# The input of chunks 1 to 3 of a hybrid decoder layer: turned by VectorE from strided loads, with the norm's factor applied at the projections' outputs

## The chip, the cores and the metric

One core of one Trainium2 chip. The metric is device time in microseconds (us); the time before is 1935.48 us, the median of 3 runs (1933.53 to 1936.48).

## The reference

One layer on 2048 rows of 1024 float32 numbers. The layer's lines that matter:

```
h  = rms_norm(x, g)                      # x * rsqrt(mean(x*x) + eps) * g
z  = h @ w_in                            # q 512 | k 128 | v 128 | b 512 | c 512 | xc 512
A  = window attention(rms_norm(q), rms_norm(k), v, sinks)   # blocks of 128, 8 heads, 2 kv heads
Cv = b * short_conv(c * xc, conv_w)      # 3 taps, per column
x  = x + concat(rms_norm(A), rms_norm(Cv)) @ w_out
x  = x + square(relu(rms_norm(x) @ w_up)) @ w_down
```

rms_norm multiplies each row by one number and each column by one number. A row's number can therefore be left out ahead of `h @ w_in` and be multiplied into the rows of the product instead.

## The kernel before

Every product of two float32 matrices runs as three matmuls on parts: a high part, rounded to TensorE's format, and a low part, the rest (`mm3`, L264 to L268: high x high, high x low, low x high). Making the parts is one cast on ScalarE and one subtraction on VectorE.

The rows are worked through in four chunks of 512 (`mixers`, called for c = 0 to 3), each of four blocks of 128 (b = 0 to 15). `h` is the chunk's normalised input, turned so that its 1024 columns lie on the partitions: two tiles (high and low) of 128 x 8 x 512 with a single buffer, so that the next chunk's h is written when the last convolution group of this chunk has read it. A chunk has these pieces:

- The convolution, `conv_pair` (L779), twice per chunk: groups of 24 matmuls of 128x512 for two column tiles each of c (`pc`), xc (`px`) and b (`pb`). The result of pc is copied out of its PSUM bank (L803 on ScalarE; in chunk 0, where the row factor is not yet in h, L805 on VectorE multiplies by the squared factor `rs0_row`).
- The output projection, `out_projection`: half 1 (the convolution's rows, `pout` with `yt`) and half 0 (the attention's, `pout` with `at`). Each result is multiplied by the norm factor of its rows (`rc` or `ra`) and added to x (L892).
- The next chunk's input, `prepare` (L364): four fetches of 128 whole rows (512 KB each) into the two buffers `xt`; `norm` (squares on ScalarE, rsqrt on GpSimd, the multiplication by row factor and gain row on VectorE, L282); then `transposed` (L288): for every 128 rows, two groups of four TensorE transposes into one PSUM bank (L294), a cast to the high part (L298) and a subtraction for the low part (L299).
- The projection to q, k and v, `project_qkv`: `pz` groups of the next chunk.
- The attention of each block: q and k norm, `qk_transpose` (transposes ptq and ptk, L638 and L640, and their parts, L643 to L648), `softmax` (scores psc, L665, copies and selects L673 and L676, exponentials L682, normalisation L690), `values` (transposes of the probabilities ptp, L701, their parts pp, L707 and L708, window masks on GpSimd, L714, then po, L753, and o, L761 on), `attn_rstd` (one matmul pa, L774).

What sets the order: `besides` yields one small step at a time of convolution, output projection, preparation and projection, and `fill(n)` runs n such steps between the pieces of attention; the numbers are in FILL. That is the program's order. Below it a list scheduler of the tile framework builds the order on each engine from its own estimates of when operands are there, and a piece may be moved forward or back by a number from PRIO (`ahead(i)`). The built order is fixed: each engine runs its instructions in that order and waits at each for what it needs. PSUM has 3 banks for projections ("mm"), 4 for attention ("at"), 1 for transposes ("tr"). All loads, and the stores of weight parts that later chunks use, are issued from SyncE's (SP's) queue in program order.

The MLP follows the mixers, from about 700 us on. Its own input is turned by `load_turned` (L312: four strided loads, 32 x 32 x 32 pieces of 128 bytes) and `turned` (L321: a VectorE transposition within blocks of 32x32, L323, then a multiplication by gain and row factor, L325). `gain_row` (L356) loads one gain for all partitions.

Of the kernel before, what the change touches and what calls it, by code (L numbers as in the profile page):

```python
# [7 lines left out]
F32 = mybir.dt.float32  # L8
# [3 lines left out]
AF = mybir.ActivationFunctionType  # L12
# [4 lines left out]
P = 128  # L17
D = 1024
# [51 lines left out]
CHP = CH + 32  # L70
STEPS = 3
TS = 32
REST = 7
LATER = 250

# [27 lines left out]
def hymba_layer(  # L103
# [23 lines left out]

    const = ctx.enter_context(tc.tile_pool(name="const", bufs=1))
    small = ctx.enter_context(tc.tile_pool(name="small", bufs=1))

    both_pool = ctx.enter_context(tc.tile_pool(name="both", bufs=1, reuse_waits="tile"))
    wop_ctx = ExitStack()
# [16 lines left out]
        for tb in range(NTB)  # L149
    ]  # L150
    rs_dram = [dram.tile([CH], F32, name=f"rs_dram{c}") for c in range(NCHUNK)]
    wds_dram = [[dram.tile([P, 2, BW], F32, name=f"wds{g}_{i}") for i in range(2)] for g in range(NCG // 2)]

    def bank(tag, name):
# [126 lines left out]
    def scaled(xt, rs, gb):  # L281
        nc.vector.scalar_tensor_tensor(xt, xt, rs, gb, op0=ALU.mult, op1=ALU.mult)  # L282

    def norm(xt, gb, name):

        scaled(xt, norm_stats(xt, name), gb)

    def transposed(xt, dst, t, name, tag="tr"):  # L288

        for kk in range(0, KD, 4):  # L290
            with ahead(9):
                pt = bank(tag, f"pt_{name}_{kk}")
                for j in range(4):
                    nc.tensor.transpose(pt[:, j * P : (j + 1) * P], xt[:, (kk + j) * P : (kk + j + 1) * P], ident)  # L294
                p3 = pt.rearrange("p (k t) -> p k t", k=4)
                dh = dst[0][:, kk : kk + 4, t * P : (t + 1) * P]
                dl = dst[1][:, kk : kk + 4, t * P : (t + 1) * P]
                nc.scalar.copy(dh, p3)  # L298
                nc.vector.tensor_tensor(dl, p3, dh.bitcast(F32), op=ALU.subtract)  # L299
            yield  # L300

    def raised(xt, dst, name, tag="tr"):

        for k in range(2):
# [59 lines left out]
    def prepare(src, r0, gb, dst, name):  # L364

        xs = []

        def fetch(t):
            xt = row("xt", f"xt_{name}_{t}", 2)
            nc.sync.dma_start(xt, src[r0 + t * P : r0 + (t + 1) * P, :])  # L370
            with ahead(8):
                norm(xt, gb, f"{name}_{t}")
                xs.append(xt)

        fetch(0)
        fetch(1)
        yield
        for t in range(NT):
            yield from transposed(xs[t], dst, t, f"{name}_{t}")
            if t + 2 < NT:  # L380
                fetch(t + 2)


    def flat(blk):
        return blk.rearrange("p k c -> p (k c)")
# [158 lines left out]
    with tc.tile_pool(name="mix_small", bufs=1) as mix_small, tc.tile_pool(name="mix", bufs=1) as mix:  # L544
# [10 lines left out]
        def project_qkv(c, h, z):  # L555
# [36 lines left out]
            w4 = [w.rearrange("p (k c) -> p k c", k=KD) for w in weights(None, c, "qkv2")]  # L592

            for pc, t in ((0, 0), (0, 1), (1, 0), (0, 2), (0, 3), (1, 1), (1, 2), (1, 3)):
                n = 256 if pc else AW
                ps = bank("mm", f"pz{c}_{pc}_{t}")[:, :n]
                hk = lambda s, k, t=t: h[s][:, k, t * P : (t + 1) * P]
                wk = (lambda s, k: w4[s][:, k, :]) if pc else (lambda s, k: both[k // (KD // 2)][s][:, k % (KD // 2), :])
                for k in range(KD):
                    mm3(ps, lambda s, k=k: hk(s, k), lambda s, k=k: wk(s, k), k == 0, k == KD - 1)  # L600
                    if (k % 2 or not pc) and k < KD - 1:
# [174 lines left out]
            nc.vector.tensor_copy(ms, pa[:, :1])  # L776
            rsqrt(dst, ms)

        def conv_pair(c, h, j, yt, ssc):  # L779

            nm = f"c{c}_{j}"

# [15 lines left out]
            for i in range(2):  # L798
                ps = bank("mm", f"pc_{nm}_{i}")
                yield from group(hl, ps, i)  # L800
                g = pool.tile([P, CHP], F32, tag="s2", name=f"u_{nm}_{i}", bufs=4)
                if c:
                    nc.scalar.copy(g[:, 2 : CH + 2], ps)  # L803
                else:
                    nc.vector.tensor_tensor(g[:, 2 : CH + 2], ps, rs0_row, op=ALU.mult)  # L805
                gc.append(g)
                yield
            hl = weights(cols256(wi, O_X + j * 256), c, f"wx{j}")
# [129 lines left out]
                    x_put(0, t, 2, b[1])  # L938
                yield

        def besides(c, before, h, yt, rc, x1, h_next, z_next):
# [11 lines left out]
            out = out_projection(c, 1, yt, rc, x1)  # L953
            if c + 1 < NCHUNK:
                h_next += parts(pool, "h", f"h{c + 1}")
                steps = prepare(xf, (c + 1) * CH, g_row[0], h_next, f"a{c + 1}")
            else:
                steps = prepare_mlp(gain_row(mlp_norm_g, "g_mlp"))
            for i, _ in enumerate(steps):
                yield  # L960
                for j in range(STEPS):
                    next(out, None)
                    yield
                    if (i, j) == PC:
# [5 lines left out]
                        ms = mix_small.tile([P, NT], F32, tag="msc", name=f"ms_c{c}", bufs=1)  # L970

                        with tc.high_priority(offset=SOON):
                            if c:
                                nc.vector.tensor_copy(ms, pc[:, :NT])
                                rsqrt(rc, ms)
                            else:
                                nc.vector.tensor_tensor(ms, pc[:, :NT], rs0_2, op=ALU.mult)
                                rsqrt(rc, ms)
                                nc.gpsimd.tensor_tensor(rc, rc, rs0, op=ALU.mult)
            yield from out  # L980
            if c + 1 < NCHUNK:
                yield from project_qkv(c + 1, h_next, z_next)
            else:
                begin_mlp()

        def mixers(c, before, h, z):


            last = c + 1 == NCHUNK
            n_fill = FILL[c]  # L990
            stage[0] = c
            at, yt, x1, h_next, z_next = [], [], [], [], []
            ra = small.tile([P, NT], F32, tag="ra", name=f"ra{c}", bufs=2)
            rc = small.tile([P, NT], F32, tag="rc", name=f"rc{c}", bufs=2)
            steps = besides(c, before, h, yt, rc, x1, h_next, z_next)
            left = out_projection(c, 0, at, ra, x1)

            spare = (NT - 1) * NCT if last else 0
# [43 lines left out]
                        attn_rstd(b, sqa, ra[:, NT - 1 : NT])  # L1042
                    yield

            return rest(), h_next, z_next

        z = []
        for _ in project_qkv(0, h, z):
# [40 lines left out]
        left = iter(())  # L1089
        for c in range(NCHUNK):  # L1090
            left, h, z = mixers(c, left, h, z)
        for _ in left:
            pass

# [479 lines left out]
```

## Time and profile before

| | |
|---|---|
| median of 3 runs | 1935.48 us (1933.53 to 1936.48) |
| the profiled execution | 1936.33 us; its span, first to last instruction, 1934.6 us; granted clock 0.999 |
| transposes of chunks 1 to 3 | 96 in 24 groups of four |
| bytes moved by DMA | 412 MB, mean 213 GB/s |

PE is TensorE, PEld its weight load, DVE is VectorE, ACT is ScalarE, POOL is GpSimd, SP is SyncE. A line of a group reads: source line, engine, operation, output <- inputs, shape, count | busy us, mean ns of one | idle us of the engine just before them and what ended it. In the timeline: start, duration (us), engine, line, operation. SPq is the part of SyncE that issues transfers. Times are from one profiled execution.

### The profile page before, as it was taken

The numbers are of one execution on the slowest core, as the hardware profiler recorded it, in microseconds if no ns is written. First come the engines' busy times: TensorE is split into PE (matmuls) and PEld (weight loads), VectorE is DVE, ScalarE is ACT, GpSimd is POOL, SyncE is SP. The second block draws the span as 40 slices with busy tenths as digits, with TensorE's granted clock in tenths as the row PEclk, the third lists the DMA queues.
The fourth block names the chain that finished last, engine by engine and source line by source line (L and its number), as shares of the span: only waits on it lengthen the run. The fifth ranks groups of instructions, "written<-read, shape, count | busy, mean of one in ns | idle before, by whom it ended". The sixth has DMA issues, their size and how long they took to land.

```text
span 1934.6 us, 24806 instructions
## 1 busy us (share of the span) xinstructions
PE 1916.7 (99%) x9025; PEld 1596.0 (82%) x9025; DVE 1206.7 (62%) x1872; ACT 837.7 (43%) x1593; POOL 273.3 (14%) x473
## 2 busy tenths in 40 slices
PE   9999999999999999999999999999999999999999
PEld 9888888888888788888877888888888888888887
DVE  4885667447556768899878766666534334448541
ACT  6563445345344437445465554554422333232220
POOL 1112203312221112222201111101000000100000
PEclk9999999999999999999999999999999999999999
DMA  9774855464474787877665544437964457776631
GB/s 324 274 261 150 288 223 188 169 255 155 163 276 170 241 299 277 250 216 249 227 222 191 180 162 143 164 123 295 376 218 151 143 163 229 262 229 219 211 135 55
DMA packets 240634, 412.25 MB, mean 213 GB/s; under 512 B 51704, under 2 KB 147968, under 8 KB 228736
## 3 DMA queue, kind: packets, MB, share of 16 engines
q1 hardware_dynamic: 211824, 335.15, 51.3%
q0 software_dynamic: 15424, 51.40, 6.8%
q10 hardware_dynamic: 13264, 24.13, 3.3%
q8 instruction: 71, 1.16, 0.2%
q14 instruction: 51, 0.42, 0.1%
HBM read 284.78 MB, written 125.83 MB: 212 GB/s over the span
## 4 chain that ended last, share of the span: by engine, by line
PE 84%; issue 5%; DVE 4%; DMA 4%; ACT 2%; POOL 1%; SPq 1%; ACTq 0%; POOLq 0%; DVEq 0%
PE d L1534 31%; PE u L1427 23%; PE pout L266 2%; PE pout L268 2%; PE pout L267 2%; PE pz L266 2%; PE pz L267 2%; PE pz L268 2%; PE pc_c L266 2%; PE px_c L266 2%; PE px_c L267 2%; PE px_c L268 2%; PE pc_c L268 2%; PE pc_c L267 2%; PE psc_b L665 1%
## 5 line engine op out<-in xcount | busy, mean ns | idle before, releaser
L1427 PE MATMUL u<-op_x,wop 128*128 128x512 f32 x2688 | 612.5, 390 | 3.0 <-DVE wop L417 1.3
L1534 PE MATMUL d<-op_w,op_f 128*128 128x512 f32 x2688 | 609.4, 389 | 0.0
L1427 PEld LDWEIGHTS u<-op_x,wop 128*128 128x128 f32 x2688 | 503.7, 188 | 111.4 <-DVE wop L417 4.0
L1534 PEld LDWEIGHTS d<-op_w,op_f 128*128 128x128 f32 x2688 | 504.7, 188 | 104.6
L398 DVE TENSOR_TENSOR op_f<-op_f 128x1024 fp32r<-128x1024 f32 x112 | 136.9, 1225 | 237.8 <-ACT op_f L397 237.4
L397 ACT CAST op_f<-op_f 128x1024 fp32r<-128x1024 f32 x112 | 118.0, 1054 | 355.9 <-DMA op_f<-fop 343.7
L416 ACT CAST wop<-wu 128x512 fp32r<-128x512 f32 x156 | 96.4, 621 | 92.0 <-PE u L1427 87.7
L417 DVE TENSOR_TENSOR wop<-wu,wop 128x512 fp32r<-128x512 f32 x156 | 111.7, 717 | 34.1 <-ACT wop L416 19.0
L1163 POOL DMA_DIRECT2D fop<-s x96 | 52.3, 545 | 433.3 <-DVE s L1166 426.4
L1169 DVE TENSOR_TENSOR u<-u,u 128x512 f32<-128x512 f32 x128 | 87.8, 686 | 18.8 <-PE u L1427 18.8
L398 DVE TENSOR_TENSOR op_w<-raw,op_w 128x1024 fp32r<-128x1024 f32 x56 | 68.4, 1222 | 25.4 <-ACT op_w L397 25.4
L397 ACT CAST op_w<-raw 128x1024 fp32r<-128x1024 f32 x56 | 58.9, 1053 | 42.3 <-PE d L1534 20.1
L1175 ACT ACTIVATE u<-u 128x512 f32<-128x512 f32 x64 | 40.6, 634 | 51.7 <-DVE u L1169 50.0
L682 ACT ACTIVATE sc_b<-sc_b,ngm_b 128x128 f32<-128x128 f32 x128 | 49.9, 392 | 26.5 <-DVE ngm_b L679 26.5
L714 POOL TENSOR_SCALAR_AFFINE_SELECT pp_b<-pp_b 128x512 fp32r<-128x512 f32 x60 | 41.1, 697 | 116.9 <-ACT pp_b L707 63.4
L1376 POOL DMA_DIRECT2D wds<-raw x16 | 8.6, 535 | 333.8 <-DVE raw L1374 333.8
L416 ACT CAST wop<-wu_s 128x512 fp32r<-128x512 f32 x64 | 39.5, 621 | 35.6 <-PE u L1427 27.4
L266 PE MATMUL pout<-w_wo,yt_c 128*128 128x512 f32 x128 | 52.4, 410 | 0.0
L268 PE MATMUL pout<-w_wo,yt_c 128*128 128x512 f32 x128 | 51.9, 406 | 0.0
L267 PE MATMUL pout<-w_wo,yt_c 128*128 128x512 f32 x128 | 51.2, 400 | 0.0
L266 PE MATMUL pout<-w_wo,at_b 128*128 128x512 f32 x128 | 50.2, 395 | 0.2 <-DVE x L892 0.2
L267 PE MATMUL pout<-w_wo,at_b 128*128 128x512 f32 x128 | 50.0, 391 | 0.3 <-DVE w_wo L249 0.3
(255 smaller groups left out, 3132.7 us busy)
## 6 DMA issues: line engine op xcount, KB each, us to landing
op_f<-fop SPq DMA_DIRECT2D x112, 512.0 KB, 4.5
raw<-in_w_down_dram SPq DMA_DIRECT2D x72, 512.0 KB, 4.4
wu<-in_w_up_dram SPq DMA_DIRECT2D x128, 256.0 KB, 3.8
w_wo<-wo SPq DMA_DIRECT2D x24, 1024.0 KB, 6.8
fop<-s POOLq DMA_DIRECT2D x96, 256.0 KB, 2.7
fop<-u ACTq DMA_DIRECT2D x64, 256.0 KB, 2.3
op_x<-xop SPq DMA_DIRECT2D x28, 512.0 KB, 6.5
w_q<-qkv SPq DMA_DIRECT2D x24, 512.0 KB, 6.0
```

The costliest lines, as they stand in the source:

```text
L266: nc.tensor.matmul(ps, st(0), mv(0), start=first, stop=False)
L267: nc.tensor.matmul(ps, st(0), mv(1), start=False, stop=False)
L268: nc.tensor.matmul(ps, st(1), mv(0), start=False, stop=last)
L397: nc.scalar.copy(op[:, 0], raw)
L398: nc.vector.tensor_tensor(op[:, 1], raw, op[:, 0].bitcast(F32), op=ALU.subtract)
L416: splits.append(nc.scalar.copy(hi, blk).ins)
L417: nc.vector.tensor_tensor(lo, blk, hi.bitcast(F32), op=ALU.subtract)
L682: nc.scalar.activation(sc[:, hd, :], sc[:, hd, :], AF.Exp, bias=ngm[:, hd : hd + 1], accum_out=den[:, hd : hd + 1])
L1163: eng.dma_start(fop_dram[tb][ORDER_DOWN.index(i)][n // 2][:, n % 2], b)
L1169: return nc.vector.tensor_tensor(dst, ps, b, op=ALU.add).ins
L1427: nc.tensor.matmul(pt, wops[i][:, a, k, :], xops[tb, p][k // 2][:, b, k % 2, :], start=p not in GOES_ON and k + j == 0, stop=k + j == NB + ...
L1534: nc.tensor.matmul(ps[tb][j], fs[tb][:, a, k, j * P : (j + 1) * P], w[:, b, k, :], start=first and p not in GOES_ON and k + n == 0, stop=l ...
```

## The change

For chunks 1 to 3, `norm` and `transposed` are gone. `load_turned` brings x itself in blocks (four jj, each two column tiles k), VectorE turns them, and the parts of h are made with the column's gain as a per-partition number, without the row factor. The squares of the rows are taken from whole rows, loaded into the same two `xt` buffers earlier, during the convolution (`stats`, one step at every 13th convolution step). The row factor `rs` is applied where the q, k, v products are copied out of PSUM, its square at pc's output (from a row of squared factors stored to memory and loaded for all partitions), and the convolution's norm factor `rc` takes both as chunk 0's did. pc's output is now multiplied on VectorE in every chunk. The k loop of `project_qkv` goes in the order 0, 4, 1, 5, ... The gain row of the attention norm is gone; its buffer holds the turned tile and the row of squared factors. `small_pad` is an unused tile.

```
-                nc.scalar.copy(dh, p3)
-                nc.vector.tensor_tensor(dl, p3, dh.bitcast(F32), op=ALU.subtract)
...
+    def turned_input(c, jj):
+
+        xt = row("xt", f"xt_a{c}_{jj}", 2)
+        load_turned(xt, xf, c * CH, jj)
+        return xt
+
+    def prepare(c, dst, gb, xts):
+
+        yield
+        for jj in range(NB):
+            for k in (jj, jj + NB):
+                xt = xts[jj][:, (k // NB) * BW : (k // NB + 1) * BW]
+                with ahead(9):
+                    dh, dl = (d[:, k] for d in dst)
+                    st = gb[:, k // NB]
+                    nc.vector.transpose(st, xt)
+                    nc.scalar.activation(dh, st, AF.Copy, scale=g_in[k])
+                    nc.vector.scalar_tensor_tensor(dl, st, g_in[k], dh.bitcast(F32), op0=ALU.mult, op1=ALU.subtract)
+                yield
+            if jj + 2 < NB:
+                xts.append(turned_input(c, jj + 2))
+
+    def stats(c, rs, xts):
+
+        rows = []
+
+        def fetch(t):
+            r = c * CH + t * P
+            rows.append(row("xt", f"xr_a{c}_{t}", 2))
+            nc.sync.dma_start(rows[t], xf[r : r + P, :])
+
+        def square(t):
+            ss = small.tile([P, 1], F32, tag="ss", name=f"ss_a{c}_{t}", bufs=2)
+            nc.scalar.activation(rows[t], rows[t], AF.Square, scale=D**-0.5, accum_out=ss)
+            rsqrt(rs[0][:, t : t + 1], ss)
+
+        with tc.issue_after(z_in[-1]) if c == 1 else nullcontext():
+            fetch(0)
+            fetch(1)
+        yield
+        square(0)
...
+        square(3)
+        nc.gpsimd.tensor_tensor(rs[1], rs[0], rs[0], op=ALU.mult)
+        nc.gpsimd.dma_start(rs2_dram[c].rearrange("(p t) -> p t", p=P), rs[1])
+        xts.append(turned_input(c, 0))
+        yield
+        xts.append(turned_input(c, 1))
...
+            KS = [i * NB + jj for jj in range(NB) for i in range(2)]
...
-                nc.scalar.copy(z[t][:, pc * AW : pc * AW + n], ps)
+                nc.scalar.activation(z[t][:, pc * AW : pc * AW + n], ps, AF.Copy, scale=rs[:, t : t + 1])
...
-                if c:
-                    nc.scalar.copy(g[:, 2 : CH + 2], ps)
-                else:
-                    nc.vector.tensor_tensor(g[:, 2 : CH + 2], ps, rs0_row, op=ALU.mult)
+                t3 = lambda a: a.rearrange("p (t q) -> p t q", t=NT)
+                nc.vector.tensor_tensor(t3(g[:, 2 : CH + 2]), t3(ps), rs2_row, op=ALU.mult)
...
             for j in range(2):
-                yield from conv_pair(c, h, j, yt, ssc)
+                for i, _ in enumerate(conv_pair(c, h, j, yt, ssc, rs2_row)):
+                    if (j * 48 + i) % STATS == 0:
+                        next(sums, None)
+                    yield
+            for _ in sums:
+                pass
...
-                steps = prepare(xf, (c + 1) * CH, g_row[0], h_next, f"a{c + 1}")
+                steps = prepare(c + 1, h_next, gb, xts)
...
+                            nc.vector.tensor_tensor(ms, pc[:, :NT], rs[1], op=ALU.mult)
+                            rsqrt(rc, ms)
+                            nc.gpsimd.tensor_tensor(rc, rc, rs[0], op=ALU.mult)
...
-        g_row = [gain_row(attn_norm_g, "g_attn")]
```

More of the change, by code (lines that the diff above doesn't have):

```diff
@@ L72 @@
 TS = 32
+STATS = 13
 REST = 7
@@ L129, in hymba_layer @@
     small = ctx.enter_context(tc.tile_pool(name="small", bufs=1))
+    small.tile([P, 48], F32, name="small_pad")
     both_pool = ctx.enter_context(tc.tile_pool(name="both", bufs=1, reuse_waits="tile"))
@@ L151, in hymba_layer @@
     rs_dram = [dram.tile([CH], F32, name=f"rs_dram{c}") for c in range(NCHUNK)]
+    rs2_dram = [dram.tile([CH], F32, name=f"rs2_dram{c}") for c in range(NCHUNK)]
     wds_dram = [[dram.tile([P, 2, BW], F32, name=f"wds{g}_{i}") for i in range(2)] for g in range(NCG // 2)]
@@ L282, in scaled @@
         nc.vector.scalar_tensor_tensor(xt, xt, rs, gb, op0=ALU.mult, op1=ALU.mult)
[L284 to L300, printed above, removed]
     def raised(xt, dst, name, tag="tr"):
@@ L362, in parts @@
         return [pool_.tile([P, KD, CH], F32R, tag=f"{tag}{s}", name=f"{tag}{s}_{name}", bufs=1) for s in range(2)]
-    def prepare(src, r0, gb, dst, name):
-        xs = []
-        def fetch(t):
[L369 to L376, printed above, removed]
-        yield
[L378 to L381, printed above, removed]
+    def turned_input(c, jj):
+        xt = row("xt", f"xt_a{c}_{jj}", 2)
+        load_turned(xt, xf, c * CH, jj)
+        return xt
@@ new lines, in stats @@
+    def stats(c, rs, xts):
+        rows = []
+        def fetch(t):
+            r = c * CH + t * P
[8 more added lines that the diff above has]
+            fetch(1)
+        yield
+        square(0)
+        yield
+        square(1)
+        fetch(2)
+        yield
+        fetch(3)
+        yield
+        square(2)
+        yield
+        square(3)
+        nc.gpsimd.tensor_tensor(rs[1], rs[0], rs[0], op=ALU.mult)
+        nc.gpsimd.dma_start(rs2_dram[c].rearrange("(p t) -> p t", p=P), rs[1])
+        xts.append(turned_input(c, 0))
+        yield
+        xts.append(turned_input(c, 1))
@@ L598, in project_qkv @@
                 wk = (lambda s, k: w4[s][:, k, :]) if pc else (lambda s, k: both[k // (KD // 2)][s][:, k % (KD // 2), :])
-                for k in range(KD):
-                    mm3(ps, lambda s, k=k: hk(s, k), lambda s, k=k: wk(s, k), k == 0, k == KD - 1)
-                    if (k % 2 or not pc) and k < KD - 1:
+                for n_k, k in enumerate(KS):
+                    mm3(ps, lambda s, k=k: hk(s, k), lambda s, k=k: wk(s, k), n_k == 0, n_k == KD - 1)
+                    if (n_k % 2 or not pc) and n_k < KD - 1:
                         yield
-                nc.scalar.copy(z[t][:, pc * AW : pc * AW + n], ps)
+                nc.scalar.activation(z[t][:, pc * AW : pc * AW + n], ps, AF.Copy, scale=rs[:, t : t + 1])
                 if pc and not t:
@@ L777, in attn_rstd, with conv_pair @@
             rsqrt(dst, ms)
-        def conv_pair(c, h, j, yt, ssc):
+        def conv_pair(c, h, j, yt, ssc, rs2_row):
             nm = f"c{c}_{j}"
@@ L939, in prepare_mlp, with besides @@
                 yield
-        def besides(c, before, h, yt, rc, x1, h_next, z_next):
+        def besides(c, before, h, yt, rc, x1, h_next, z_next, rs, rs_next):
             yield from before
             ssc = mix.tile([P, CH], F32, tag="ssc", name=f"ssc{c}", bufs=1)
-            for j in range(2):
-                yield from conv_pair(c, h, j, yt, ssc)
+            gb = pool.tile([P, 2, CH], F32, tag="gb", name=f"gb{c}", bufs=1)
+            rs2_row = rs0_row.rearrange("p (t q) -> p t q", t=NT)
+            if c:
+                nc.sync.dma_start(gb[:, 0], rs2_dram[c].partition_broadcast(P))
+                rs2_row = gb[:, 0].rearrange("p (q t) -> p t q", t=NT)
+            if c + 1 < NCHUNK:
+                rs_next += [small.tile([P, NT], F32, tag=f"rs_a{i}", name=f"rs{i}_a{c + 1}", bufs=2) for i in range(2)]
+            xts = []
+            sums = stats(c + 1, rs_next, xts) if c + 1 < NCHUNK else iter(())
+            for j in range(2):
+                for i, _ in enumerate(conv_pair(c, h, j, yt, ssc, rs2_row)):
+                    if (j * 48 + i) % STATS == 0:
+                        next(sums, None)
+                    yield
+            for _ in sums:
+                pass
             x1 += [] if c else x0
@@ L972, in besides, with mixers @@
                         with tc.high_priority(offset=SOON):
[L973 to L979, printed above, removed]
+                            nc.vector.tensor_tensor(ms, pc[:, :NT], rs[1], op=ALU.mult)
+                            rsqrt(rc, ms)
+                            nc.gpsimd.tensor_tensor(rc, rc, rs[0], op=ALU.mult)
             yield from out
             if c + 1 < NCHUNK:
-                yield from project_qkv(c + 1, h_next, z_next)
+                yield from project_qkv(c + 1, h_next, z_next, rs_next[0])
             else:
                 begin_mlp()
-        def mixers(c, before, h, z):
+        def mixers(c, before, h, z, rs):
             last = c + 1 == NCHUNK
@@ L991, in mixers @@
             stage[0] = c
-            at, yt, x1, h_next, z_next = [], [], [], [], []
+            at, yt, x1, h_next, z_next, rs_next = [], [], [], [], [], []
             ra = small.tile([P, NT], F32, tag="ra", name=f"ra{c}", bufs=2)
             rc = small.tile([P, NT], F32, tag="rc", name=f"rc{c}", bufs=2)
-            steps = besides(c, before, h, yt, rc, x1, h_next, z_next)
+            steps = besides(c, before, h, yt, rc, x1, h_next, z_next, rs, rs_next)
             left = out_projection(c, 0, at, ra, x1)
@@ L1043, in rest @@
                     yield
-            return rest(), h_next, z_next
+            return rest(), h_next, z_next, rs_next
         z = []
@@ L1087, in hymba_layer @@
             nc.gpsimd.memset(vd[:, kv, 1, 1 - kv, :].bitcast(F32), 0.0)
-        g_row = [gain_row(attn_norm_g, "g_attn")]
-        left = iter(())
+        left, rs = iter(()), [rs0, rs0_2]
         for c in range(NCHUNK):
-            left, h, z = mixers(c, left, h, z)
+            left, h, z, rs = mixers(c, left, h, z, rs)
         for _ in left:
```

2 lines of the change are left out of this document (1 added, 1 removed).

## The prediction, made before the changed kernel ran

> **What bounds the kernel now.** I read the page first, then the busy time by stretches, then what TensorE waits for.
>
> ```profile
> span 1934.6 us, 24806 instructions
> PE 1916.7 (99%) x9025; PEld 1596.0 (82%) x9025; DVE 1206.7 (62%) x1872; ACT 837.7 (43%) x1593; POOL 273.3 (14%) x473
> ```
>
> TensorE (PE) is the bound: 99% of the span. The change touches only the mixers, the first 700 us or so. The windows view of that part (length, then PE, PE weight loads, VectorE, ScalarE, GpSimd busy, granted clock, DMA share, GB/s):
>
> ```profile
> 60.00:90.00 30.00, 30.00 (x152) 25.28 (x151) 27.27 (x63) 17.77 (x50) 4.38 (x8) 1.00 0.85 295
> 90.00:125.00 35.00, 35.00 (x171) 29.13 (x170) 29.37 (x59) 21.17 (x61) 2.56 (x8) 1.00 0.71 265
> 125.00:160.00 35.00, 32.92 (x178) 27.16 (x177) 29.84 (x59) 21.24 (x56) 7.97 (x14) 1.00 0.76 263
> ```
>
> PE hardly ever stops, and VectorE (DVE) is the next busiest, 27 of 30 us in one stretch. So PE loses time only through more or fewer instructions of its own, or through a wait that other matmuls do not cover. The attention transposes of before show that cover: groups by line (busy us, mean ns, then idle before them).
>
> ```profile
> L701 PE MATMUL ptp_b<-ident,sc_b 128*128 128x128 f32 x128 | 28.9, 271 | 0.0
> L753 PE MATMUL po_b<-pp_b,vz 128*128 128x512 f32 x64 | 22.8, 408 | 0.0
> L665 PE MATMUL psc_b<-kw,qt_b 128*128 128x256 f32 x240 | 41.0, 284 | 0.6 <-ACT sc_b L673 0.4
> ```
>
> These 432 matmuls, which depend on what ScalarE (ACT), DVE or GpSimd (POOL) made just before, cost 0.6 us of waiting in all, because projection matmuls stand between them in PE's queue.
>
> **What goes.** The 96 transposes of chunks 1 to 3.
>
> ```profile
> L294 PE MATMUL pt_a<-ident,xt_a 128*128 128x128 f32 x96 | 14.8, 277 | 4.0 <-DVE h_h L299 1.7 <-DVE ms_b L776 1.2 <-DVE xt_a L282 1.1
> ```
>
> The timeline shows what four of them take from PE:
>
> ```profile
> 124.46 0.40 PE L267 MATMUL pout<-w_wo,yt_c 128*128 128x512 f32 x1
> 124.69 0.39 PE L268 MATMUL pout<-w_wo,yt_c 128*128 128x512 f32 x1
> ...
> 124.92 0.60 PE L294 MATMUL pt_a<-ident,xt_a 128*128 128x128 f32 x4
> ...
> 125.28 0.48 PE L266 MATMUL pout<-w_wo,yt_c 128*128 128x512 f32 x1
> ...
> 125.59 0.40 PE L267 MATMUL pout<-w_wo,yt_c 128*128 128x512 f32 x1
> ```
>
> Matmuls follow each other by 0.23. The four push the next one from 124.92 to 125.28 (0.36), and the one behind it starts 0.31 later instead of 0.23 (0.08): 0.44 a group, 24 groups, **-10.6 us**. With the 4.0 us of waits in front of them, **-14.6 us** at most.
>
> **What is added beside PE.**
>
> ```profile
> L298 ACT CAST h_h<-pt_a 128x512 fp32r<-128x512 f32 x24 | 14.0, 584 | 21.1 <-PE pt_a L294 21.0
> L299 DVE TENSOR_TENSOR h_h<-pt_a,h_h 128x512 fp32r<-128x512 f32 x24 | 16.5, 690 | 4.7 <-ACT h_h L298 4.3
> L282 DVE SCALAR_TENSOR_TENSOR xt_a<-xt_a,rs_a,g_attn 128x1024 f32<-128x1024 f32 x12 | 16.1, 1344 | 4.9 <-POOL rs_a L191 4.9
> L323 DVE STREAM_TRANSPOSE st_m<-xt_r 128x512 f32<-128x512 f32 x16 | 10.9, 698 | 0.0
> L248 ACT ACTIVATE w_wo<-raw_wo,g_y 128x512 fp32r<-128x512 f32 x16 | 10.8, 724 | 0.1
> L249 DVE SCALAR_TENSOR_TENSOR w_wo<-raw_wo,g_y,w_wo 128x512 fp32r<-128x512 f32 x16 | 11.6, 746 | 0.0
> L325 DVE SCALAR_TENSOR_TENSOR st_m<-st_m,g_cols,rs_rest 128x512 f32<-128x512 f32 x16 | 19.0, 1190 | 0.0
> L817 DVE TENSOR_TENSOR u_c<-px_c,u_c 128x512 f32<-128x512 f32 x16 | 11.0, 688 | 17.5 <-PE px_c L268 17.5
> L803 ACT COPY u_c<-pc_c 128x512 f32<-128x512 f32 x12 | 7.1, 589 | 12.6 <-PE pc_c L268 12.4
> ```
>
> DVE loses 16.5 + 16.1 = 32.6 us. It gains 24 turns (the L323 operation, 16.8), 24 low parts (as L249, 17.9) and 12 multiplications of pc by the turned factor row. No row of before has that multiplication; L325 reads the same kind of rearranged row and takes 1.19; the plain product of L817 takes 0.69. I take 1.19, to which it is nearest: 14.3 us (8.3 by the other end). It comes some 48 matmuls, 11 us, before the px product that needs it. Net +16 us on an engine with idle time. ACT loses 14.0 + 7.1 and gains 24 x 0.724 = 17.4; its 12 squares stay. The factor at pz rides on a copy that was there; the extra POOL multiplication at rc and the stored squared factor are small and early (the squares run during the convolution, the factor is used a chunk later). What hides them all is the matmul stream, as long as it is fed; I count 0, with bounds of -1 and +3, the upper one being three chunks at one late part of h (0.75 + 0.25).
>
> **DMAs.** Each of chunks 1 to 3 gets 16 turned loads of 128 KB beside its row loads. Before has the same load in the MLP; one line each of the source view, the queue table and the issue list (window 765 to 835):
>
> ```profile
> L317 SPq DMA_DIRECT2D xt_r<-x_dram x32: 562/664/3944, 765.2 to 905.5; - x32
> q1 hardware_dynamic: 25996, 8.65, 50.1%
> xt_r<-x_dram SPq DMA_DIRECT2D x16, 128.0 KB, 4.2
> ```
>
> 25996 packets took 50.1% of 16 engines for 70 us: 0.0216 us of one engine each. A turned load is 1024 pieces of 128 B, so 1.4 us of all 16 engines, 22 us a chunk. Eight of them stand on SP's queue in chunk 0 between the load of the raw x weights and that of the raw b weights (second pair), and so ahead of the stores that free weight buffers: 11 us. Stretches 60 to 160 leave 0.15 x 30 + 0.29 x 35 + 0.24 x 35 = 23 us of DMA free, so I cost them at 0, upper end +11. The Trainium skill's page "DMA: Bandwidth & Descriptors", section Specifications, names 512 B as the least transfer for full rate, and so speaks against these loads. By its fabric ceiling of 435 GB/s four turned loads (512 KB) would take an estimated 1.2 us of all engines. The trace sides with the rule on pieces: 5.5 us by the packets above.
>
> **What moves.** This carries the forecast. The built kernels have a fixed instruction order on each engine, readable without running. The MLP's order is the same in both. In the mixers the changed kernel no longer spreads the attention of a block between projection matmuls, but packs it. The first place, PE in order:
>
> ```
> before: ptp_b0, px, ptp_b0, px, ptp_b0, px x2, px, ptp_b0_1, px, ... (4+4 ptp among 12 px), px x13,
>         po_b0, px x3, ptq_b2, ptk_b2, po_b0, px x12, pb x18, psc_b2 x16
> after:  ptp_b0 x8, po_b0 x2, ptq_b2 x4, po_b0, ptk_b2, po_b0, psc_b2 x13, px x4, psc_b2 x3, ptp_b1_0 x4, px
> ```
>
> Before, some 30 projection matmuls lie between ptp_b0 and ptq_b2; after, none. PE is in order, so it waits out the chain. Its links:
>
> ```profile
> L707 ACT CAST pp_b<-ptp_b 128x512 fp32r<-128x512 f32 x32 | 18.2, 587 | 33.6 <-PE ptp_b L701 32.9 <-POOL pp_b L714 0.6
> L708 DVE TENSOR_TENSOR pp_b<-ptp_b,pp_b 128x512 fp32r<-128x512 f32 x32 | 21.2, 686 | 20.1 <-ACT pp_b L707 20.0
> L643 ACT CAST qt_b<-ptq_b 64x512 fp32r<-64x512 f32 x32 | 18.6, 583 | 16.8 <-PE ptq_b L638 9.2 <-DVE qt_b L644 6.6 <-PE psc_b L665 0.5
> L644 DVE TENSOR_TENSOR qt_b<-ptq_b,qt_b 64x512 fp32r<-64x512 f32 x32 | 22.0, 688 | 5.9 <-ACT qt_b L643 5.3
> L673 ACT COPY sc_b<-psc_b 128x256 f32<-128x256 f32 x64 | 23.1, 373 | 38.5 <-PE psc_b L665 35.7
> L676 DVE COPY_PREDICATED sc_b<-later,psc_b 128x128 f32<-128x128 int32 x120 | 28.0, 299 | 17.9 <-ACT sc_b L673 17.8
> L714 POOL TENSOR_SCALAR_AFFINE_SELECT pp_b<-pp_b 128x512 fp32r<-128x512 f32 x60 | 41.1, 697 | 116.9 <-ACT pp_b L707 63.4 <-PE po_b L753 42.5 <-DVE pp_b L708 10.2
> L682 ACT ACTIVATE sc_b<-sc_b,ngm_b 128x128 f32<-128x128 f32 x128 | 49.9, 392 | 26.5 <-DVE ngm_b L679 26.5
> L690 DVE TENSOR_TENSOR sc_b<-sc_b,den_b 128x1024 f32<-128x1024 f32 x16 | 19.6, 1223 | 0.3
> ```
>
> Place 1, worked out: four ptp 0.6; cast 0.59; low part 0.69 (1.9), its second half 0.65 (2.5); ptq 0.6 and qt cast by 3.1; two qt parts on ACT and DVE in turn with the kw parts between them, 2.5 (5.6); psc 0.6; score copy 0.37 and two selects 0.6 before the bank comes free (7.1); once more 0.5 (7.6); the x weight's cast stands behind these copies on ACT (0.59, 8.2) and the last scores behind four such casts (10.6). PE's own work there is 5.5, so about **5.5** stand idle. The other places by the same links:
>
> - 2, chunk 0, end of pb: block 1's o, block 3's q, k and scores, all ahead of pout: 7.9
> - 3, chunk 0, between pout: block 2's p and o, then the second out weight's low part behind two turns and two low parts of h: 4.5
> - 4, chunk 0: block 3's p and o: 1.9
> - 5, chunk 1, last pb: block 5's p, then q of block 7: 3.1
> - 6, chunk 1: pc1 right behind the sum of squares: 1.3
> - 7, chunk 1, between pout: p and o of blocks 6 and 7 with three pout between. po_b6 waits for a cast that stands behind eight exponentials (0.39 each) and two high parts of h (0.72 each); ptp_b7 for the normalisation (1.22); pa_b7 for its squares behind two turns: 11.7
> - 8, chunk 2, the same kind for blocks 9 to 11: 9.1
>
> Sum 45.0. Chunk 3 is about as before. From it I take off 3, by choice, because each stall lets ACT and DVE catch up before the next place: **+42**. Bounds: 21 (half of the links already done when PE arrives) to 49 (0.19 more for each of some twenty exponentials, if their sums' readout is not overlapped).
>
> **Sum.** Profiled execution 1936.33 (span 1934.6, 1.7 around it): -14.6 + 42 = +27.4, 1963.7; the median of the runs shown is 0.85 lower, so **1962.9, say 1963**. With 21: 1942. With 49 and +3: 1973.
>
> **Rivals.**
> 1. *Faster: the packed order hides.* PE arrives at the packed places only when ACT and DVE have done their part, so only the removal is left: 1935.5 - 14.6 = 1921; each place left at what place 4 costs (1.9 x 8 = 15) gives 1936. It decides at 14.6 us of stalls, 1.8 a place. For it: each wait before was covered. Against: in place 1 the producer is PE's own transpose a microsecond earlier, and nothing else is queued.
> 2. *The turned loads bind.* The raw b weights come 11 us late. In before, load and use are these:
>
> ```profile
> 86.47 0.38 SPq L239 DMA_DIRECT2D raw_wb<-in_w_in_dram  x1
> 111.18 0.39 PE L266 MATMUL pb_c<-h_a,w_wb 128*128 128x512 f32 x1
> ```
>
> From 86.5 to 111.2 are 24.7 us, for a load of several us and the split; 11 us of delay would nearly use up what is left. If nothing is left, the forecast grows by 11: 1974. Place 1's own stall pushes pb later and speaks against it.
> 3. *DVE binds.* In stretches 60 to 160 it is 84 to 91% busy; chunk 0 gets a third of +16, 5 us, less than the 13.5 us that it has idle there. If all of it lands on chains, 1963 + 5 = 1968.
> 4. *Nothing changes:* stalls equal the saving, within 0.2% of 1935.5.
>
> **Chances.** Forecast 0.62, its own range 1942 to 1973; rival 1 0.17; rival 2 0.12; rival 3 0.05; rival 4 0.04. A measurement of this kernel tells about 0.2% from no change. Faster by more than that: 0.17; within it: 0.04; slower: 0.62 + 0.12 + 0.05 = 0.79. The range leaves out some 0.10 at the lower end of rival 1 (below 1926) and some 0.08 where rival 2 or 3 meets the upper bound of the stalls (above 1980): 1926 to 1980.
>
> **What would show it.** Right: pt_a gone and PE busy lower by about 15 us; PE's waits naming pp_b, qt_b, sc_b, o_b, w_wx and w_wo in stretches around 97 to 150, 270 to 320 and 460 to 480, some 40 us more idle in the mixers; the MLP as long as before. Wrong: the mixers' PE as full as before (rival 1); PE waiting for a weight part whose own wait is a DMA (rival 2); ptp and po spread between projections, which would mean that the order isn't the one that I read.

## The result, and the profile after

The changed kernel takes 2000.12 us (median of 4 runs, 1995.66 to 2000.36) beside 1935.98 for the kernel before: ratio 1.0327, 95% interval 1.0308 to 1.0345. It is slower, as forecast, but by 64 us where 27 were forecast, and outside the range. The profiled execution took 1995.66 us, its span 1994.0; the other three took 4.4 to 4.7 us more, at a granted clock of 0.984 to 0.986 instead of 0.988.

The page of the changed kernel, the lines that answer to those shown of before, and the granted clock by slices (a digit is tenths of full speed):

```profile
span 1994.0 us, 24719 instructions
...
PE 1932.8 (97%) x8929; PEld 1598.9 (80%) x8929; DVE 1218.9 (61%) x1896; ACT 832.0 (42%) x1581; POOL 278.0 (14%) x482
...
PEclk9989999899999999999999999999999999999999
```

PE has 96 instructions fewer and is busy 16 us longer. That can't be work; it is matmuls that take longer. The mixers end where the first `u` matmul starts: at 695.4 us before, at 751.9 after. The windows view, split there, first of before and then of after (length, PE, PE weight loads, DVE, ACT, POOL busy, granted clock, DMA share, GB/s):

```profile
0.00:695.40 695.40, 684.42 (x3602) 578.91 (x3603) 442.05 (x897) 328.60 (x873) 146.14 (x262) 1.00 0.63 226
```

```profile
0.00:751.90 751.90, 698.57 (x3506) 580.88 (x3506) 453.40 (x921) 323.42 (x861) 150.40 (x271) 0.97 0.64 218
751.90:1994.00 1242.10, 1234.23 (x5424) 1017.99 (x5424) 765.54 (x976) 508.54 (x721) 127.65 (x211) 1.00 0.61 205
```

56.5 of the 59.4 us lie in the mixers. There PE's idle time grew from 695.40 - 684.42 = 11.0 to 751.90 - 698.57 = 53.3 us, by 42.3; its busy time grew by 14.2 although work was taken away; and the clock fell from 1.00 to 0.97. What PE waited for in the changed kernel (total, times, longest):

```profile
PE po_b L775 <- ACT pp_b L729: 7.5, 7, 3.0
PE pout L270 <- DVE w_wo L252: 5.3, 3, 2.4
PE psc_b L687 <- DVE qt_b L666: 4.9, 3, 2.3
PE pa_b L796 <- DVE o_b L791: 4.8, 2, 4.2
PE ptq_b L660 <- DVE z L649: 4.5, 2, 2.3
PE pz L270 <- DMA w_q<-qkv: 3.6, 1, 3.6
```

These are the links named in the prediction (pp, qt, o, the out weight's low part), and two that were not: the norm of q and k (z) and a DMA. How they look at place 2, in PE's timeline:

```profile
131.50 0.60 PE L723 MATMUL ptp_b<-ident,sc_b 128*128 128x128 f32 x4
131.85 0.71 PE L775 MATMUL po_b<-pp_b,vz 128*128 128x512 f32 x2
132.40 0.63 PE L775 MATMUL po_b<-pp_b,vd 128*128 128x512 f32 x2
134.81 0.60 PE L775 MATMUL po_b<-pp_b,vz 128*128 128x512 f32 x1 [1.78 <-ACT pp_b L729]
135.21 1.06 PE L660 MATMUL ptq_b<-ident,z 128*128 128x128 f32 x4
136.06 0.42 PE L662 MATMUL ptk_b<-ident,z 128*128 128x128 f32 x1
136.31 1.87 PE L1001 MATMUL pc<-mean,ssc 128*128 128x1 f32 x8
140.43 1.23 PE L687 MATMUL psc_b<-kw,qt_b 128*128 128x256 f32 x4 [2.25 <-DVE qt_b L666]
...
144.01 2.34 PE L687 MATMUL psc_b<-kw,qt_b 128*128 128x256 f32 x12
```

The packed attention, with nothing of a projection to fill its waits. From 135 on the same instructions also take longer: four transposes 1.06 us where they took 0.60 at 131.5. The clock column of the windows there says why:

```profile
130.00:135.00 5.00, 3.22 (x18) 2.40 (x17) 3.71 (x8) 3.25 (x7) 0.99 (x3) 1.00 1.01 427
135.00:140.00 5.00, 3.18 (x14) 2.73 (x13) 3.65 (x9) 3.17 (x9) 1.92 (x3) 0.51 0.43 179
140.00:145.00 5.00, 4.57 (x15) 3.99 (x16) 3.46 (x9) 3.40 (x7) 1.11 (x3) 0.50 0.25 40
145.00:150.00 5.00, 4.96 (x25) 3.97 (x24) 4.97 (x9) 5.00 (x12) 0.00 (x0) 0.97 0.92 276
```

For ten us TensorE ran at half speed.

### The profile page after: what moved, and what is told of

Read it like the earlier page. It is cut to its first block, busy times and chain, and to the rows that moved or that the text cites. A ratio compares the mean times of both kernels' runs of the same rounds, so it can differ in the third digit from the quotient of the medians.

```text
span 1994.0 us, 24719 instructions
## 1 busy us (share of the span) xinstructions
PE 1932.8 (97%) x8929; PEld 1598.9 (80%) x8929; DVE 1218.9 (61%) x1896; ACT 832.0 (42%) x1581; POOL 278.0 (14%) x482
## 4 chain that ended last, share of the span: by engine, by line
PE 81%; issue 5%; DVE 5%; DMA 4%; ACT 2%; POOL 2%; SPq 1%; POOLq 0%; DVEq 0%; ACTq 0%
PE d L1563 31%; PE u L1456 24%; PE pout L269 2%; PE pout L270 2%; PE pout L271 2%; PE pz L269 1%; PE pz L270 1%; PE pz L271 1%; PE pc_c L269 1%; PE pc_c L271 1%; PE pc_c L270 1%; PE psc_b L687 1%; PE px_c L269 1%; PE px_c L271 1%; PE px_c L270 1%
```

## The experiments

The theory: the change's loads and operations cost little; their place on SyncE's queue leads the scheduler to pack the attention, PE waits out each packed place, and behind the waits the granted clock halves. Rivals: the 128-byte pieces; VectorE's added work; the waits alone, without the clock.

### The order, with all of the change's work kept

```
-        load_turned(xt, xf, c * CH, jj)                 # nc.sync.dma_start inside
+        load_turned(xt, xf, c * CH, jj, nc.gpsimd)      # nc.gpsimd.dma_start instead
```

> The changed kernel with one edit: its turned loads are issued from GpSimd's queue instead of SyncE's. Loads, pieces and all arithmetic stay; the built order spreads most of chunk 0's attention between projection matmuls again. Theory (the packed order, and the clock that drops behind its waits, make the loss): TensorE's idle time in the mixers falls from 53 us to 15 to 30, the granted clock from 0.97 back to 0.99 or more, the time to 1925 to 1955. Rival (the 128-byte pieces load the DMA engines, or VectorE's added work binds): both are still there, so 1985 to 2005.

Measured 1947.38 us (ratio 1.0058, 1.0042 to 1.0075). In the mixers:

```profile
0.00:702.90 702.90, 683.81 (x3505) 574.85 (x3505) 455.81 (x921) 322.90 (x861) 185.42 (x319) 0.98 0.67 233
```

Idle 19 us instead of 53, and some 53 us less time. The order is the spread one: at place 1 the eight ptp stand among px matmuls from 103.59 us on and the first po comes at 110.65, while in the changed kernel eight ptp, po and ptq follow each other from 98.48 on with no px between. VectorE's work is the same, so it can account for no more than the 11 us that this kernel still lies above the one before.

Of the pieces this run says less. A load is still 1024 pieces of 128 bytes, but the packets differ: the DMA view has 2432 packets for the 6.30 MB of GpSimd's queue, 2.6 KB each, where the changed kernel has 57648 packets under 512 bytes beside 7598 before. What speaks against them is who waited for a DMA. From 30 us to the end of the changed kernel's mixers PE did so for 4.9 us in all. ScalarE and VectorE together did so for 36 us, where the kernel before had 28, and never for a turned tile. These 4.9 and 8 us don't make up PE's 42 us of added waits.

### Whole rows in place of the turned loads

```
-        load_turned(xt, xf, c * CH, jj)
+        for pg in range(4):
+            r = c * CH + jj * P + pg * TS
+            nc.sync.dma_start(xt[pg * TS : (pg + 1) * TS], xf[r : r + TS, :])
```

> The changed kernel with the turned loads replaced by as many loads of whole rows (4 KB pieces) from the same queue; the input of chunks 1 to 3 is then not the turned one, all else is computed as before. The built order is spread again here too. Theory of the order: about what the kernel with the loads on GpSimd's queue takes, within 10 us, 1925 to 1950. Rival of the small pieces: clearly faster than that kernel, since here alone the pieces are gone: that one above 1980, this one below 1950.

Measured 1948.49 us (1.0065, 1.0047 to 1.0083): as the one above, with 4 KB pieces instead of 128 bytes. Place 1 is spread here too (the first ptp stand among px at 102.07), with as many loads at the same place on SyncE's queue. So the place alone doesn't pack the order; it takes the turned loads in that place. Why the scheduler answers so is not shown. Neither this run nor the last has the 128-byte packets, so the two don't price them.

### The kernel before, with a packed order

```
-    (40, 0, 160, -10, 10, 0, 80, ...),      # PRIO, chunk 0; entries 4 and 5 are the values' steps
-    (220, 0, -60, -50, 40, 0, 270, ...),
-    (200, 0, 10, -50, 40, 0, 260, ...),
+    (40, 0, 160, -10, 500, 500, 80, ...),
+    (220, 0, -60, -50, 500, 500, 270, ...),
+    (200, 0, 10, -50, 500, 500, 260, ...),
```

> The kernel before with one edit: priority offset 500 for the probabilities and for the products with the values in chunks 0 to 2 (it was 10 or 40, and 0). Transposes, loads and arithmetic are those of before; the built order packs each block's ptp and po. Theory of the order: slower by idle time of some 20 to 40 us and by a lower clock behind it, 1960 to 1995. Rival (the loss comes from what the change loads and computes): within 10 us of 1936.

Measured 1984.21 us (1.0247, 1.0232 to 1.0262). Nothing of the change is in it, and 48 us are lost:

```profile
0.00:741.60 741.60, 704.56 (x3602) 584.82 (x3603) 439.39 (x897) 326.96 (x873) 144.97 (x262) 0.98 0.59 212
```

Idle 37 us instead of 11, busy 20 more for the same 3602 instructions. The order alone makes a loss of this size. It is packed otherwise than the changed kernel's: the longest waits here are for x ahead of pout (8.4 us), z (6.4) and the scores (5.6).

### Without the row loads and squares

```
     def stats(c, rs, xts):
+        nc.gpsimd.tensor_copy(rs[0], rs0)
+        nc.gpsimd.tensor_copy(rs[1], rs0_2)
+        nc.gpsimd.dma_start(rs2_dram[c].rearrange("(p t) -> p t", p=P), rs[1])
+        xts.append(turned_input(c, 0))
+        xts.append(turned_input(c, 1))
+        return
```

> The changed kernel without the row loads and squares of chunks 1 to 3; their row factor is chunk 0's, so the output differs. The turned loads stay on SyncE's queue. The built order spreads again, though chunk 0's first turned loads come earlier. Theory of the order: 1930 to 1960. Rival (turned loads of small pieces bind): 1980 or more, as they all remain.

Measured 1959.97 us (1.0128, 1.011 to 1.0147), idle 712.2 - 684.6 = 28 us in the mixers. The small-piece loads are all there on SyncE's queue (57457 packets under 512 bytes), and the time is 20 us below the least that was expected if they bound. Since the run also removes work and changes the order, it limits what the pieces can cost, to the 24 us above the kernel before, and doesn't price them.

### A spread order in all chunks, and the queue alone

The numbers of PRIO, FILL and STATS were set anew for a spread order with the turned loads on GpSimd's queue; then the same numbers with the loads back on SyncE's.

```
-STATS = 13
+STATS = 10
-    (40, 0, 160, -10, 10, 0, 80, 10, -20, 30, 0, 300),
-    (220, 0, -60, -50, 40, 0, 270, -20, 50, 280, 0, 0),
-    (200, 0, 10, -50, 40, 0, 260, -20, 70, 280, 0, 10),
-    (200, 20, 180, -10, 0, 0, 40, 40, -20, 0, 0, 30),
+    (40, 0, 70, -40, 10, 0, -100, 10, -20, 20, 0, 0),
+    (250, 0, 0, -50, 0, 0, 0, -20, 50, 0, 0, 0),
+    (20, -100, 10, 0, 40, 0, 260, -20, 70, 0, 40, 70),
+    (260, 10, 180, 0, 0, 0, 40, 40, -20, 0, 0, 100),
...
-        load_turned(xt, xf, c * CH, jj)
+        load_turned(xt, xf, c * CH, jj, nc.gpsimd)
```

> The changed kernel with the turned loads on GpSimd's queue and with other numbers in PRIO, FILL and STATS (10 instead of 13), chosen so that the built order spreads the attention of all chunks. Nothing that it loads or computes differs. Theory of the order: what is left is the gain forecast for the removal, 10.6 to 14.6 us, less a few us of other waits: 1921 to 1932, TensorE idle in the mixers 10 to 18 us, clock 0.99 or more. Rival (VectorE's added work or the small pieces cost something whatever the order): 1940 or more.

Measured 1932.70 us (median of 11 runs; 0.998, 0.997 to 0.999, to the kernel before): the fastest of all, a fifth of a per cent better than before.

```profile
0.00:685.50 685.50, 674.27 (x3505) 571.21 (x3506) 453.33 (x922) 324.81 (x862) 184.16 (x317) 1.00 0.68 238
685.50:1929.60 1244.10, 1233.78 (x5425) 1018.15 (x5423) 763.36 (x975) 507.25 (x720) 127.15 (x213) 1.00 0.61 205
```

The mixers are 9.9 us shorter than before: idle 11.2 (11.0), PE busy 10.1 less. That is the removal, 10.6 by the sum, without the 4.0 of waits. Half comes back later: the MLP takes 1244.1 us instead of 1239.2.

> The same numbers in PRIO, FILL and STATS, but the turned loads back on SyncE's queue, ahead of the stores of weight parts; the built order is packed again in chunks 0 to 2. Theory (place on SyncE's queue decides the order, and the order the time): 1985 to 2005, as the changed kernel. Rival (the numbers of PRIO and FILL alone were what the changed kernel lacked): 1920 to 1945.

Measured 1995.32 us (1.0299, 1.0285 to 1.0313), idle 48 us in the mixers; at place 1 eight ptp, po and ptq follow each other again, from 100.87 on. One queue for another, and 63 us. Since the kernel before with a packed order loses as well, I read this as the built order's doing; this pair alone can't tell it from what the loads do on SyncE's queue itself.

### The price of a wait

```
     def load_op(src, name, raw=None, early=False, slow=0):
+        for _ in range(slow):
+            nc.scalar.copy(raw, raw)
         nc.scalar.copy(op[:, 0], raw)
```

> The kernel before; in the down projection, at three steps out of 56 (20, 30 and 40), the raw weight is copied onto itself 71, 65 and 50 times on ScalarE ahead of its cast, so that TensorE waits a few us in a stretch that holds nothing but matmuls of one shape. The result is unchanged. Theory of the clock: behind each wait of over some 3 us the granted clock falls for several us, and the time grows by more than the idle time, by 1.3 to 1.8 times. Rival (a wait costs its length; the low clock of the changed kernel comes from something else): time and idle time grow alike, clock 1.00.

Measured 1955.89 us (1.0097, 1.0083 to 1.011). The profiled span grew by 1950.0 - 1934.6 = 15.4, PE's added waits are 12.3:

```profile
PE d L1537 <- ACT op_f L400: 8.4, 2, 7.8
PE d L1537 <- DVE op_f L401: 2.1, 1, 2.1
PE d L1537 <- DVE d L1462: 1.8, 1, 1.8
```

The longest, in the timeline and in windows:

```profile
1646.78 0.61 PE L1537 MATMUL d<-op_w,op_f 128*128 128x512 f32 x2
1655.22 9.00 PE L1537 MATMUL d<-op_w,op_f 128*128 128x512 f32 x31 [7.83 <-ACT op_f L400]
```

```profile
1645.00:1647.00 2.00, 2.00 (x10) 1.66 (x9) 2.00 (x2) 1.94 (x3) 0.00 (x0) 1.00 0.00 0
...
1652.00:1655.00 3.00, 0.00 (x0) 0.00 (x0) 0.00 (x0) 0.88 (x1) 0.00 (x0) 0.50 1.03 421
1655.00:1658.00 3.00, 2.78 (x7) 2.20 (x8) 2.80 (x3) 3.00 (x5) 0.00 (x0) 0.50 1.03 422
1659.00:1662.00 3.00, 3.00 (x14) 2.44 (x13) 3.00 (x3) 3.00 (x4) 0.00 (x0) 1.00 0.58 229
...
1772.00:1774.00 2.00, 2.00 (x6) 1.52 (x6) 2.00 (x4) 2.00 (x3) 0.00 (x0) 0.50 0.58 223
1775.00:1778.00 3.00, 3.00 (x15) 2.47 (x14) 3.00 (x7) 0.00 (x0) 0.00 (x0) 1.00 0.00 0
```

PE stops at 1647.4; the clock is half from 1652, and full again by 1659, less than 4 us after PE restarts at 1655.2. At half speed those 3.5 us cost another 1.8. The waits of 1.8 and 2.1 us, two matmuls apart, did the same (the last two rows); the wait of 0.60 us, at 1538, cost its length. Time over idle is 15.4 / 12.3 = 1.25, a little under the 1.3 expected. That is the fastest of the four executions, at a granted clock of 0.996; the others had 0.993 to 0.994, and by the medians the kernel takes 1955.89 - 1936.56 = 19.3 us more, so 1.25 is the low end. The Trainium skill's page "TensorE: Matmul & The Clock Gate", section "What's actually happening", describes a free-running window of some 3.4 us in which activity is judged, half speed after an idle one and full speed after a busy one. The long wait agrees with it. The two short ones go beyond its words: each is under 3.4 us, and matmuls ran between them.

### More matmuls in the packed places

```
+        def keep_warm(ps, n):
+            for _ in range(n):
+                nc.tensor.matmul(ps[:, :P], ident, ident, start=True, stop=True)
...
+                    keep_warm(ps, WARM_PO.get((b, kv), 0))      # ahead of po; so for psc and pa
```

> The changed kernel with 140 useless matmuls (identity by identity, 128x128, into the bank whose real product comes next) ahead of the products that wait longest in the packed places of chunks 0 to 2; the result is unchanged, the order round them shifts a little. Theory (the packed waits cost their length and a half clock behind them): useful work is not sooner ready, but TensorE no longer falls quiet, so the granted clock rises from 0.97 to 0.985 or more in the mixers and the time falls by 8 to 20 us in spite of 140 matmuls more: 1980 to 1992. Rival (the waits alone cost): 2000 to 2014.

Measured 1983.62 us (1.0243, 1.0226 to 1.0259): 16.5 us faster than the changed kernel, with more work. A useless matmul shows as two records; their groups and the mixers' window:

```profile
L643 PE MATMUL po_b<-ident 128*128 128x128 f32 x172 | 21.5, 276 | 0.0
L643 PE MATMUL psc_b<-ident 128*128 128x128 f32 x64 | 8.1, 277 | 2.8 <-DVE qt_b L673 2.2 <-DVE sc_b L707 0.6
L643 PE MATMUL pa_b<-ident 128*128 128x128 f32 x44 | 5.6, 275 | 0.0
```

```profile
0.00:735.40 735.40, 711.39 (x3786) 602.74 (x3786) 455.25 (x921) 323.53 (x861) 150.33 (x271) 1.00 0.66 222
```

Idle and useless together are 24.0 + 35.2 = 59 us, no less than the 53 idle before; the order round the fillers moved a little. But without the useless groups PE's busy time is 711.4 - 35.2 = 676.2 us instead of 698.6, with the clock at 1.00. Not all of these 22 us are clock, since a useless matmul also runs over the end of the useful one ahead of it. The clock's own part can be read in the changed kernel. These are the stretches of its mixers, behind the first 30 us, in which the clock was low:

```profile
104.00:108.00 4.00, 3.85 (x16) 3.43 (x17) 1.35 (x6) 2.63 (x6) 0.00 (x0) 0.57 0.01 2
135.00:146.00 11.00, 8.75 (x35) 7.61 (x35) 8.08 (x18) 7.57 (x16) 3.03 (x5) 0.53 0.37 109
165.00:170.00 5.00, 4.38 (x12) 3.48 (x13) 4.94 (x8) 1.25 (x5) 0.00 (x0) 0.66 0.20 55
189.00:194.00 5.00, 5.00 (x15) 3.95 (x16) 0.44 (x2) 0.00 (x0) 0.00 (x0) 0.66 1.01 418
353.00:357.00 4.00, 3.11 (x10) 2.28 (x10) 2.45 (x6) 1.86 (x5) 2.73 (x4) 0.57 1.09 384
363.00:371.00 8.00, 3.86 (x11) 3.21 (x12) 3.90 (x8) 2.18 (x4) 1.43 (x4) 0.57 0.00 0
541.00:545.00 4.00, 3.58 (x10) 2.67 (x10) 4.00 (x8) 1.38 (x5) 3.16 (x4) 0.57 0.98 321
729.00:733.00 4.00, 4.00 (x15) 3.27 (x14) 3.40 (x6) 1.07 (x3) 2.34 (x4) 0.57 0.93 295
```

PE's busy time in each, times what the clock lacks of 1.00, adds up to 15.2 us. So the low clock is worth some 15 us in the changed kernel, a cost of its own beside the waits; the profiled span of the filled kernel is shorter by as much (1994.0 - 1979.0 = 15.0).

The trace also shows when waits cost clock. By windows of 1 us the eight spells begin at 104.36, 135.08, 165.80, 189.68, 353.52, 363.76, 541.26 and 729.00 us. These times lie whole multiples of 3.413 us apart, and each spell lasts one, two or three such steps. When the mixers behind the first 30 us are cut into these steps, every step at full clock in which PE was busy for 1.67 us or less is followed by half clock, and none in which it was busy for 1.70 or more. Three waits of 2.2 us fell in steps with 1.70, 1.75 and 2.14 us of work (from 206.8, 397.9 and 421.8 on) and cost only their length. The line is not as sharp everywhere: in the kernel with the loads on GpSimd's queue, three steps with 1.97 to 2.78 us of work were followed by half clock.

### The removed transposes, doubled

```
-                for j in range(4):
+                for j in range(8):
+                    j %= 4
                     nc.tensor.transpose(pt[:, j * P : (j + 1) * P], ...)
```

> The kernel before with each group of four transposes of chunks 1 to 3 issued twice into the same bank (96 more). By the sum of the removal (0.44 us for four): 10.6 us more, with up to 5 us of waits by the order: 1946 to 1952. If the transposes were covered, under 1940; if they cost their busy time of 0.6 us and more, 1952 or more.

Measured 1952.92 us (1.0082, 1.0068 to 1.0096), 16.4 more than before, just past the range that the sum gave and, by the time alone, on the side of the dearer transposes. The trace says where it comes from. The mixers are 17.4 us longer (712.8 us): idle is 14.3 us (3.3 more), and PE is busy 14.1 us more, of which some 5 are half clock (three spells, in windows of 1 us). The timeline has eight in a row:

```profile
127.17 1.04 PE L295 MATMUL pt_a<-ident,xt_a 128*128 128x128 f32 x8
127.96 0.47 PE L268 MATMUL pout<-w_wo,yt_c 128*128 128x512 f32 x1
```

The next matmul starts 0.79 us after them, twice the 0.36 of four and a little. Without waits and clock the 96 transposes cost some 9 us, so the excess over 10.6 is not a dearer transpose.

### The last chunk's order

In the spread kernel the last rows of PRIO and FILL were set back to those of before.

> The kernel with the spread order (turned loads on GpSimd's queue) with the numbers of PRIO and FILL of its last chunk set back to those of before. In that kernel the mixers were 9.9 us shorter and the MLP 4.9 us longer than in the kernel before. If its last chunk's order delays the MLP's first loads, the MLP is back at about 1240 and the time 1928 to 1931; if the MLP's start is bound by its loads whatever the order, nothing is gained: 1931 to 1936.

Measured 1935.92 us (0.9996, 0.9987 to 1.0004). Mixers 692.9, MLP 1242.1: the MLP got 2 us back and the mixers lost 7. What lengthens the MLP's start when the mixers end sooner is not settled; in the spread kernel its longest wait there is 3.6 us for a cast on ScalarE, which itself stands behind a load of op_x, and half clock follows for 3.4 us from 729.6 on.

## Why the prediction was wrong in size

- **The direction and its cause held.** The packed order was read from the built kernel, and PE waited for the links named: pp, qt, o and the out weights, and for under 1 us each kw and the squares.
- **The removal held.** -10.6 was forecast for the transposes, 10.1 less busy time was measured where the order is spread. The further -4.0 of waits did not come: idle was 11.2 against 11.0.
- **The sum of the waits held, its places only in part.** Forecast +42 of waits and -4.0 of old ones; measured +42.3 idle. But the eight places hold 28 us (length less PE's busy time in these windows of the changed kernel):

```profile
95.00:112.00 17.00, 13.70 (x66) 10.86 (x65) 10.11 (x23) 9.41 (x26) 0.85 (x1) 0.90 0.50 211
130.00:150.00 20.00, 15.93 (x69) 13.10 (x68) 15.78 (x31) 14.83 (x32) 4.02 (x7) 0.74 0.65 230
158.00:172.00 14.00, 9.96 (x34) 6.74 (x33) 11.65 (x24) 8.80 (x29) 3.68 (x7) 0.88 0.22 63
...
300.00:350.00 50.00, 46.47 (x233) 37.76 (x231) 41.24 (x89) 25.96 (x77) 9.79 (x17) 1.00 0.48 157
350.00:372.00 22.00, 13.80 (x44) 9.18 (x45) 14.63 (x30) 10.38 (x23) 9.21 (x14) 0.77 0.45 159
...
520.00:560.00 40.00, 35.05 (x159) 27.18 (x158) 29.17 (x63) 17.79 (x49) 8.36 (x12) 0.96 0.65 209
```

  That is 3.3 at place 1 (5.5 forecast), 4.1 at 2 (7.9), 4.0 at 3 (4.5), 0.4 at 4 (1.9), 3.5 at 5 and 6 (4.4), 8.2 at 7 (11.7), 5.0 at 8 (9.1). The clock column falls in the same windows: part of what I counted as standing idle was spent in PE's own work at half speed. Some 17 us were in no place of mine: 4.5 for the next chunk's q weights (the DMA wait above), two waits of 2.3 for the q and k norm ahead of ptq, 2.9 for out weights in half 0, 2.2 for x ahead of pout, and 3 more at the start of the MLP's input. The other 8 us of the 53 lie elsewhere, 4 of them in the first 30 us. That the sum came out is partly chance.
- **The step that failed: a wait was priced at its length.** A clock of 1.00 stood in every row of before, and I carried it over, at no cost. In the changed kernel PE's matmuls took 24.3 us longer (698.57 against 674.27 in the spread kernel, same instructions). Some 15 of these are half clock, in the eight spells above: behind places 1, 2, 3, 7 (two) and 8, behind the q weights and at the MLP's input. Places 5 and 6 cost no clock. The other 9 us no run separates. An estimate for most of them: a matmul of 128x512 takes 0.39 us while the next starts 0.23 behind it, so one ahead of a wait shows some 0.16 more, and with some 35 waits more than in the spread kernel that is 6 us. The profiled span grew by -10.1 + 42.3 + 24.3 in the mixers and 2.9 in the MLP, 59.4 in all; the forecast was 27.4. Of the 32 us missed, 24 are this step, 4 the old waits that were to go, 3 the MLP.
- **Rival 2** (loads bind) came true in a corner: 4.5 us of DMA waits, at the q weights and not at raw b. q weights landed after 7.7 us instead of 6.0 (medians). The prediction's price of 0.0216 us for a 128-byte piece was too high: it is the mean of the MLP's packets of all sizes, 333 bytes each. In the mixers the hardware queue took 63.6% of 751.9 us instead of 62.5% of 695.4, so the 48 loads took some 44 us of all 16 engines where 66 were counted. **Rival 3** (VectorE binds) fell: its busy time grew by 12.2 us, not 16; the multiplication by the squared factor took 1.06 us, not 1.19.
- **Rival 1** (faster) was right about the change and wrong about this build of it: with a spread order the gain is there, 0.2%.

## What to carry to other kernels

A change of loads can cost more through the order that a scheduler builds round them than through the loads: compare the built orders, and look for dependent short products that have lost the long ones between them. Price a wait of TensorE at its length, and then look at its busy time in steps of 3.41 us: where it fell to half a step or less, the changed kernel ran the next step at half clock, which costs up to 1.7 us. Where the steps begin is known only from a trace. Before judging such a change, give it an order of its own: one queue for another was worth 63 us here.

## What the hardware did that I had not expected

- Short waits halve the clock: at place 2 it fell 0.3 us behind a wait of 1.78 us, and with a second wait of 2.25 us and 14 short instructions between, half speed lasted ten us. In that kernel the work within a step of 3.41 us decided, not the length of one wait.
- Useless matmuls in the waits paid: 140 of them, 35 us of TensorE time, made the kernel 16.5 us faster.
- The turned loads came in other packets from GpSimd's queue: 2.6 KB each instead of 128 bytes, and some 26 us of all 16 DMA engines (3.7% of 702.9 us) instead of 44.
